# One hybrid mixer layer: order of the first loads, of the weight splits, and the way the modulation's row groups are summed

## The chip, the cores and the metric

One core of a Trainium2 chip. The metric is the device time of one execution in microseconds (us). It is given as the median of three runs, and a separate profiled execution gives the trace.

## What is computed

One layer in float32 with 1024 tokens of width 1024. From c comes a modulation, from x by RMS normalisation h; h is projected to all inputs of three mixers and to their gates:

```python
mod = jnp.einsum('bd,de->be', jax.nn.silu(c), w_ada) + b_ada
shift, scale, gate = jnp.split(mod[:, None, :], 3, axis=-1)
h = rms_norm(x, g_pre) * (1.0 + scale) + shift
proj = jnp.einsum('bsd,de->bse', h, w_in)
...
o_gla = rms_norm(o_gla, g_gla_norm.reshape(GLA_HEADS, GLA_VAL_DIM))
...
return x + gate * rms_norm(out, g_post)
```

The mixers are a forgetting attention (fox), a chunked gated linear attention (gla) and a causal pooling (pool). Each is gated, projected and merged, and one output projection follows.

## The kernel before

Every float32 matrix product is made of three matmuls (`mm3`, lines 143 to 145): operands are split in a high part rounded on ScalarE (line 109) and the rest, a subtraction on VectorE (line 111; both in `split`), and high by high, high by low and low by high are summed. A product of 128x512 in the text is one such matmul.

The kernel is written in a framework that orders the instructions of each engine itself by the program's order, its dependencies and priorities. So where lines are written is a wish; the order in which each engine gets its instructions is what the scheduler makes of it, and it may change far from the edited lines.

The start goes as follows. SyncE issues loads of 512 KB: `load_mod(0)`, the four tiles wa of the first modulation's weights (line 258), `load_x`, the eight tiles xn of x with 128 tokens each (line 274), and `start_w`, the weights wr_gq and wr_gk of the first two projections (line 278). `norm_x(g)` (lines 294 to 306) handles two tiles of x: sums of squares on ScalarE (line 301, Square) or VectorE (line 298), a root on ScalarE (line 303), a reciprocal and the scaling of xn on VectorE (lines 304, 306). `transpose_x` (lines 308 to 317) turns them on TensorE by 128x128 (line 313, into px) and copies to xT on ScalarE (line 315) or VectorE (line 317).

`gemv(j)` (lines 323 to 337) multiplies sc, the silu of c, by four tiles wa. It runs 32 matmuls of 256 columns (line 329) whose results stand in four groups of 32 equal rows of pr, one group for each of four parts of the sum. ScalarE copies pr to ar (line 332), and four matmuls with a column c32 of 1/32 (line 336) sum over all 128 rows, which adds the four groups, and turn the result into pt. `modulation(j)` adds biases and makes the shift and scale of two tiles of h, `gate(u)` those of the output's gate. `modulate(kt)` (lines 353 to 363) makes one tile of h for all tokens, hh (high) and hl (low), by a scale and shift on VectorE (line 361) and a split. `split_w` splits wr_gq and wr_gk into wh and wl; wnr is a third, narrow weight.

`first_products(kt)` (lines 412 to 419) multiplies tile kt of h with the three weights: 16 matmuls into ps_gq, ps_gk and ps_n. All eight tiles give 128. The next phase begins with ps_gv (lines 166 to 168), projections and then the gated linear attention in four units of `gla_unit`: matmuls psc (line 636) give scores, VectorE selects them into scs (lines 624, 628), and pso (line 658) multiplies them with the values. At a unit's end the sums of squares pm (line 694) go to VectorE (msq, line 696), and `rms_gla` (lines 700 to 713) takes a root on ScalarE, a reciprocal on VectorE (line 702) and splits the result rr into a high and a low part. The high part is multiplied by a selecting matrix into pb at line 710, the low part at line 711. Products of other projections (ps_zg, ps_fv, pp_zg) stand between them on TensorE wherever the scheduler put them.

Of the kernel before, what the change touches and what calls it, by code (L numbers as in the profile page):

```python
# [8 lines left out]
F32 = mybir.dt.float32  # L9
# [3 lines left out]
ALU = mybir.AluOpType  # L13
AX = mybir.AxisListType
PSUM = bass.MemoryType.PSUM

P = 128
# [12 lines left out]
def kernel(  # L30
# [22 lines left out]
    V, A, G, T = nc.vector, nc.scalar, nc.gpsimd, nc.tensor  # L53
# [9 lines left out]
    def open_pool(name, **kw):  # L63
        stack = ExitStack()
        return stack.enter_context(pool(name, **kw)), stack
# [7 lines left out]
    def halves():  # L73
        return ((0, slice(0, HALF)), (1, slice(HALF, S)))
# [7 lines left out]
    def bank(tag, name, shape=(P, HALF)):  # L82
        if tag == "acc":
            return ps_acc.tile(list(shape), F32, tag="acc", name=name, bufs=2)
        return ps_acc.tile(list(shape), F32, tag=tag, name=name, bufs=BANKS[tag])
# [18 lines left out]
    def const(shape, name, dt=F32):  # L104
        return cst.tile(shape, dt, tag=name, name=name)


    def split(raw, hi, lo, scale=1.0, E=None):
        i = A.activation(hi, raw, AF.Copy, scale=scale)  # L109
        if scale == 1.0:  # L110
            j = (E or V).tensor_tensor(out=lo, in0=raw, in1=hi.bitcast(F32), op=ALU.subtract)  # L111
        else:
            j = V.scalar_tensor_tensor(  # L113
                out=lo, in0=raw, scalar=scale, in1=hi.bitcast(F32), op0=ALU.mult, op1=ALU.subtract
            )
        return i, j
# [80 lines left out]
    ident = const([P, P], "ident")  # L197
    make_identity(nc, ident)
    c32 = const([P, 1], "c32")
# [8 lines left out]
    modc = const([P, 3, NK], "modc")  # L208
# [25 lines left out]
    st_pool, st_stack = open_pool("start", side="right")  # L234
# [16 lines left out]
    def load_wa(cols):  # L251

        parts = {}
        for z in range(2):
            for kh in range(2):
                t = sh((GT + ["t"] * 3 + XT[0:2])[ring[0] % 9], f"wa{len(wa)}{z}{kh}", (P, 4, 256))
                ring[0] += 1
                nc.sync.dma_start(t, w_ada[0, kh * 512 : (kh + 1) * 512, cols[z] : cols[z] + 256].rearrange(
                    "(k p) e -> p k e", p=P))
                parts[z, kh] = t  # L260
        wa.append(parts)

    def load_mod(j):

        load_wa((j * 256, D + j * 256))
# [6 lines left out]
    def load_x(a, b):  # L272
        for st in range(a, b):
            nc.sync.dma_start(xn[st], x[0, st * P : (st + 1) * P, :])

    def start_w(col, name, tags):
        raw = wtile(("wh", "wl")[name == "gk0"], f"wr_{name}", F32)
        nc.sync.dma_start(raw, w_in[0, :, col : col + P].rearrange("(k p) e -> p k e", p=P))
        hi = sh(tags[0], f"wh_{name}", (P, NK, P), F32R)
        lo = sh(tags[1], f"wl_{name}", (P, NK, P), F32R)  # L280
        return raw, hi, lo

    load_mod(0)
    load_x(0, 4)
    wq = start_w(C_GQ, "gq0", ("x3", "x4"))
    load_x(4, 8)
    wk = start_w(C_GK, "gk0", ("x5", "x2"))


# [3 lines left out]
    def norm_x(g):  # L293
        sl = slice(2 * g, 2 * g + 2)
        for st in (2 * g, 2 * g + 1):
            junk = hp.tile([P, D], F32, tag=f"hh{5 + st % 2}", name=f"junk{st}")
            if st in (3, 5, 7):
                V.tensor_tensor_reduce(out=junk, in0=xn[st], in1=xn[st], scale=1.0, scalar=0.0,
                                       op0=ALU.mult, op1=ALU.add, accum_out=ss[:, st : st + 1])
            else:  # L300
                A.activation(junk, xn[st], AF.Square, accum_out=ss[:, st : st + 1])
        V.tensor_scalar(out=ss[:, sl], in0=ss[:, sl], scalar1=1.0 / D, scalar2=EPS, op0=ALU.mult, op1=ALU.add)
        A.activation(ss[:, sl], ss[:, sl], AF.Sqrt)
        V.reciprocal(ss[:, sl], ss[:, sl])
        for st in (2 * g, 2 * g + 1):
            V.tensor_scalar(out=xn[st], in0=xn[st], scalar1=ss[:, st : st + 1], scalar2=None, op0=ALU.mult)

    def transpose_x(hf, k0, k1):
        hs = slice(hf * HALF, (hf + 1) * HALF)
        for kt in range(k0, k1):  # L310
            px = bank((("a", "a", "c", "c"), ("c", "c", "acc", "acc"))[hf][kt % 4], f"px{kt}{hf}")
            for j in range(4):
                T.transpose(px[:, j * P : (j + 1) * P], xn[4 * hf + j][:, kt * P : (kt + 1) * P], ident)
            if kt % 2 == 0:
                A.copy(xT[kt][:, hs], px)
            else:
                V.tensor_copy(xT[kt][:, hs], px)

    def split_w(w):
        raw, hi, lo = w  # L320
        split(raw, hi, lo)

    def gemv(j):

        pr = bank("b", f"pr{j}", (P, 2, 256))
        for z in range(2):
            for kh in range(2):
                for k in range(4):
                    T.matmul(pr[32 * k : 32 * k + 32, z, :], sc[:, 4 * kh + k : 4 * kh + k + 1].to_broadcast([P, 32]),  # L329
                             wa[j][z, kh][:, k, :], start=(kh == 0), stop=(kh == 1))  # L330
        ar = st_pool.tile([P, 4, P], F32, tag="ar", name=f"ar{j}", bufs=2)
        A.copy(ar, pr.rearrange("p z (c e) -> p (z c) e", e=P))

        pt = bank("d", f"pt{j}", (P, 4))
        for i in range(4):
            T.matmul(pt[:, i : i + 1], ar[:, i, :], c32, start=True, stop=True)
        return pt

    def modulation(j):
        pt = gemv(j)  # L340
        js = slice(2 * j, 2 * j + 2)
        mc = st_pool.tile([P, 2], F32, tag="mc", name=f"mc{j}", bufs=2)
        V.tensor_tensor(out=modc[:, 0, js], in0=pt[:, 0:2], in1=bsh[:, js], op=ALU.add)
        V.tensor_tensor(out=mc, in0=pt[:, 2:4], in1=bsc[:, js], op=ALU.add)
        V.tensor_tensor(out=modc[:, 1, js], in0=mc, in1=gpre[:, js], op=ALU.mult)

    def gate(u):
        pt = gemv(4 + u)
        us = slice(4 * u, 4 * u + 4)
        V.tensor_tensor(out=modc[:, 2, us], in0=pt, in1=bgt[:, us], op=ALU.add)  # L350
        V.tensor_tensor(out=modc[:, 2, us], in0=modc[:, 2, us], in1=gpost[:, us], op=ALU.mult)

    def modulate(kt):
        hh.append(hp.tile([P, S], F32R, tag=f"hh{kt}", name=f"hh{kt}"))
        hl.append(hp.tile([P, S], F32R, tag=f"hl{kt}", name=f"hl{kt}"))
        for hf, hs in halves():
            ht = xT[kt][:, hs]
            if kt == NK - 1:

                ht = st_pool.tile([P, HALF], F32, tag="ht", name=f"ht{hf}", bufs=2)  # L360
            V.tensor_scalar(out=ht, in0=xT[kt][:, hs], scalar1=modc[:, 1, kt : kt + 1],
                            scalar2=modc[:, 0, kt : kt + 1], op0=ALU.mult, op1=ALU.add)
            split(ht, hh[kt][:, hs], hl[kt][:, hs])
# [5 lines left out]
    cv, bsh, bsc, gpre = colv[:, 0:8], colv[:, 8:16], colv[:, 16:24], colv[:, 24:32]  # L369
# [2 lines left out]
    V.scalar_tensor_tensor(out=sc8, in0=th8, scalar=1.0, in1=cv, op0=ALU.add, op1=ALU.mult)  # L372
    V.tensor_scalar(out=sc, in0=sc8, scalar1=0.5, scalar2=None, op0=ALU.mult)
    V.tensor_scalar(out=bsc, in0=bsc, scalar1=1.0, scalar2=None, op0=ALU.add)
    modulation(0)
    for g in range(2):
        norm_x(g)
    transpose_x(0, 0, NK)
    for g in range(2, 4):
        norm_x(g)  # L380
    split_w(wq)
    transpose_x(1, 0, 2)
    modulate(0)
    split_w(wk)


# [34 lines left out]
    for kt in range(NK):  # L421
        if kt in (0, 2, 4):
            modulation(kt // 2 + 1)
        if kt == 0:
            load_mod(3)
        elif kt in (2, 4):
            load_gate(kt // 2 - 1)
        if kt in (5, 7):
            gate((kt - 5) // 2)
        if kt + 1 < NK:  # L430
            modulate(kt + 1)
        first_products(kt)
# [827 lines left out]
    for st in range(8):  # L1260
# [17 lines left out]
        r = yp.tile([P, 1], F32, tag="r", name=f"r{st}", bufs=2)  # L1278
# [44 lines left out]
```

## Time and profile before

| what | us |
|---|---|
| median of three runs (lowest, highest) | 1117.84 (1116.75, 1120.27) |
| profiled execution | 1116.32 |
| its span on the core | 1114.6 |
| TensorE busy in the span | 1067.6 |
| VectorE busy | 754.9 |
| ScalarE busy | 455.4 |
| GpSimd busy | 389.6 |

The mean granted clock of TensorE is 0.989 of full speed in the profiled execution. Times in a timeline are from the start of the span. The time of an execution is 1.7 us longer than its span. PE is TensorE, DVE VectorE, ACT ScalarE and POOL GpSimd; a row names output <- inputs, and a name's buffer numbers are left out.

### The profile page before, as it was taken

The numbers are of one execution on the slowest core, as the hardware profiler recorded it, in microseconds if no ns is written. First come the engines' busy times: TensorE is split into PE (matmuls) and PEld (weight loads), VectorE is DVE, ScalarE is ACT, GpSimd is POOL, SyncE is SP. The second block draws the span as 40 slices with busy tenths as digits, with TensorE's granted clock in tenths as the row PEclk, the third lists the DMA queues.
The fourth block names the chain that finished last, engine by engine and source line by source line (L and its number), as shares of the span: only waits on it lengthen the run. The fifth ranks groups of instructions, "written<-read, shape, count | busy, mean of one in ns | idle before, by whom it ended". The sixth has DMA issues, their size and how long they took to land.

```text
span 1114.6 us, 15450 instructions
## 1 busy us (share of the span) xinstructions
PE 1067.6 (96%) x5621; PEld 864.1 (78%) x5621; DVE 754.9 (68%) x1413; ACT 455.4 (41%) x859; POOL 389.6 (35%) x336
## 2 busy tenths in 40 slices
PE   4999999999999899899999999999999999999997
PEld 3679888988777788688888888887776776787886
DVE  5646979675698877987757566557675669487323
ACT  5335454443552433243434444435543337343111
POOL 1022326123075245445656454431210434343000
PEclk9999998999999999999999999999999899999999
DMA  9930110222142343146763334369969562464232
GB/s 316 306 106 6 54 39 22 67 66 74 49 130 72 137 169 113 38 162 238 255 214 113 114 118 129 113 156 346 262 201 279 208 174 86 162 216 141 77 113 76
DMA packets 97488, 159.26 MB, mean 143 GB/s; under 512 B 7978, under 2 KB 71036, under 8 KB 97412
## 3 DMA queue, kind: packets, MB, share of 16 engines
q1 hardware_dynamic: 97060, 157.47, 44.5%
q8 instruction: 44, 0.72, 0.3%
q10 hardware_dynamic: 352, 0.80, 0.2%
q14 instruction: 32, 0.26, 0.1%
HBM read 113.13 MB, written 45.13 MB: 142 GB/s over the span
## 4 chain that ended last, share of the span: by engine, by line
PE 71%; DVE 11%; DMA 10%; issue 2%; ACT 2%; POOL 2%; SPq 1%; DVEq 0%; ACTq 0%; POOLq 0%
PE pp_m L143 7%; PE pp_m L145 7%; PE pp_m L144 7%; PE pso L1275 3%; PE pso L1274 3%; PE po L1133 3%; PE pso L1273 3%; PE psy L143 2%; PE psy L145 2%; PE psy L144 2%; PE psc L636 2%; PE tp L1123 2%; PE ps_gv L168 1%; PE ps_gv L166 1%; PE ps_gv L167 1%
## 5 line engine op out<-in xcount | busy, mean ns | idle before, releaser
L143 PE MATMUL psy<-ogh,wh_y 128*128 128x512 f32 x192 | 76.2, 403 | 6.3 <-DMA ogh<-ogh_d 4.1
L145 PE MATMUL psy<-ogh,wl_y 128*128 128x512 f32 x192 | 74.5, 397 | 2.0 <-DVE wl_y L113 2.0
L144 PE MATMUL psy<-ogl,wh_y 128*128 128x512 f32 x192 | 76.0, 396 | 0.0
L143 PE MATMUL pp_m<-hh,w_m 128*128 128x512 f32 x192 | 74.7, 389 | 0.0
L144 PE MATMUL pp_m<-hl,w_m 128*128 128x512 f32 x192 | 74.7, 389 | 0.0
L145 PE MATMUL pp_m<-hh,w_m 128*128 128x512 f32 x192 | 74.7, 389 | 0.0
L111 DVE TENSOR_TENSOR w_m<-wr_m,w_m 128x512 fp32r<-128x512 f32 x36 | 42.8, 1193 | 41.6 <-ACT w_m L109 41.6
L1029 POOL TENSOR_SCALAR_AFFINE_SELECT Fd<-F 128x128 f32<-128x128 f32 x64 | 22.3, 353 | 128.1 <-DVE mx L1051 90.5
L1058 ACT ACTIVATE t<-t,ng 128x1024 f32<-128x1024 f32 (+3 forms) x64 | 49.6, 777 | 37.9 <-DVE ng L1056 35.1
L111 DVE TENSOR_TENSOR w_m<-S_m,w_m 128x512 fp32r<-128x512 f32 x48 | 57.2, 1221 | 3.3 <-ACT w_m L109 2.7
L770 POOL TENSOR_TENSOR sb<-hh,hl 128x512 f32<-128x512 f32 x16 | 23.5, 1493 | 100.6 <-PE pr L329 70.5
L1046 DVE CUSTOM_DVE_ANT_0 t<-psL,F 128x512 f32<-128x512 f32 (+2 forms) x80 | 41.2, 524 | 21.6 <-PE psL L1043 9.4
L547 POOL TENSOR_TENSOR e<-cum 128x256 f32<-128x256 f32 x24 | 19.4, 807 | 93.0 <-ACT ko L580 26.4
L1274 PE MATMUL pso<-wol,mh 128*128 128x512 f32 (+1 forms) x136 | 51.2, 377 | 0.0
L1273 PE MATMUL pso<-woh,mh 128*128 128x512 f32 (+1 forms) x136 | 51.2, 376 | 0.0
L1275 PE MATMUL pso<-woh,ml 128*128 128x512 f32 (+1 forms) x136 | 51.0, 376 | 0.0
L934 ACT ACTIVATE o_m<-o_m 128x512 f32<-128x512 f32 x48 | 29.0, 629 | 53.8 <-DVE o_m L835 31.5
L1277 DVE TENSOR_TENSOR yo<-pso,gb 128x512 f32<-128x512 f32 (+1 forms) x17 | 11.2, 661 | 55.6 <-ACT jk L1276 55.6
L143 PEld LDWEIGHTS psy<-ogh,wh_y 128*128 128x128 f32 x192 | 36.5, 191 | 15.0 <-DMA ogh<-ogh_d 4.4
L1125 ACT COPY PT<-tp 128x512 f32<-128x512 f32 (+1 forms) x64 | 31.6, 504 | 39.6 <-PE tp L1123 36.2
L1123 PE MATMUL tp<-ident,t 128*128 128x128 f32 x288 | 45.7, 280 | 1.9 <-ACT t L1058 1.1
L1133 PE MATMUL po<-PT,vf 128*64 128x256 f32 (+1 forms) x320 | 45.5, 366 | 0.0
(579 smaller groups left out, 3357.8 us busy)
## 6 DMA issues: line engine op xcount, KB each, us to landing
wa<-in_w_ada_dram SPq DMA_DIRECT2D x24, 512.0 KB, 7.2
wr_m<-in_w_in_dram SPq DMA_DIRECT2D x24, 512.0 KB, 3.7
m_d<-o_m SPq DMA_DIRECT2D x24, 512.0 KB, 8.2
m_in<-m_d SPq DMA_DIRECT2D x24, 512.0 KB, 5.4
xn<-in_x_dram SPq DMA_DIRECT2D x8, 512.0 KB, 8.4
kl<-fkl_d SPq DMA_DIRECT2D x16, 256.0 KB, 10.1
kk<-fkh_d SPq DMA_DIRECT2D x16, 256.0 KB, 5.8
F<-fc_d SPq DMA_DIRECT2D x8, 512.0 KB
```

What stands on the lines that cost most here:

```text
L111: j = (E or V).tensor_tensor(out=lo, in0=raw, in1=hi.bitcast(F32), op=ALU.subtract)
L143: T.matmul(ps, wh, rh, start=first, stop=False)
L144: T.matmul(ps, wh, rl, start=False, stop=False)
L145: T.matmul(ps, wl, rh, start=False, stop=last)
L1046: V.tensor_tensor_reduce(out=t[:, c0:e], in0=ps[:, : e - c0], in1=Fb[p, h][:, c0:e], scale=1.0, scalar=-3e38, op0=ALU.subtract, op1=ALU.ma ...
L1058: A.activation(t[:, :W], t[:, :W], AF.Exp, bias=ng[:, 0:1], accum_out=sm)
L1123: T.transpose(tp[:, j, :], t[:, kb * P : (kb + 1) * P], ident)
L1125: A.copy(pts[h, kg][:, 0:nb, qs], tp[:, 0:nb, :])
L1133: T.matmul(po[64 * h : 64 * h + 64, q0:256], vf[p // 2, kb // 4][:, kb % 4, col : col + 64], pts[h, kb // 4][:, kb % 4, q0:256], start=(kb ...
L1273: T.matmul(ps[:, :w], mh[k][:, sl], hi, start=(k == 0), stop=False)
L1274: T.matmul(ps[:, :w], mh[k][:, sl], lo, start=False, stop=False)
L1275: T.matmul(ps[:, :w], ml[k][:, sl], hi, start=False, stop=(k == NK - 1))
```

## The change

All eight tiles of x are loaded first, then the four wa, then wr_gq and wr_gk. In `gemv` four transposes take the place of the four matmuls with c32; the result, 128 columns for each of the four, is read by a reduction on VectorE that takes one column of every 32 and adds the four. In the program's order `transpose_x(1, 0, 2)`, `modulation(0)` and `modulate(0)` are written behind the normalisation of x, and both `split_w` behind `modulate(0)`.

```diff
--- before.py
+++ after.py
@@ -280,10 +280,9 @@
         lo = sh(tags[1], f"wl_{name}", (P, NK, P), F32R)
         return raw, hi, lo
 
+    load_x(0, 8)
     load_mod(0)
-    load_x(0, 4)
     wq = start_w(C_GQ, "gq0", ("x3", "x4"))
-    load_x(4, 8)
     wk = start_w(C_GK, "gk0", ("x5", "x2"))
 
 
@@ -331,18 +330,19 @@
         ar = st_pool.tile([P, 4, P], F32, tag="ar", name=f"ar{j}", bufs=2)
         A.copy(ar, pr.rearrange("p z (c e) -> p (z c) e", e=P))
 
-        pt = bank("d", f"pt{j}", (P, 4))
+        pt = bank("d", f"pt{j}", (P, 4, P))
         for i in range(4):
-            T.matmul(pt[:, i : i + 1], ar[:, i, :], c32, start=True, stop=True)
-        return pt
+            T.transpose(pt[:, i, :], ar[:, i, :], ident)
+        mc = st_pool.tile([P, 4], F32, tag="mc", name=f"mc{j}", bufs=2)
+        V.tensor_reduce(mc, pt.rearrange("p a (g r) -> p a g r", r=32)[:, :, :, 0], axis=AX.X, op=ALU.add)
+        return mc
 
     def modulation(j):
         pt = gemv(j)
         js = slice(2 * j, 2 * j + 2)
-        mc = st_pool.tile([P, 2], F32, tag="mc", name=f"mc{j}", bufs=2)
         V.tensor_tensor(out=modc[:, 0, js], in0=pt[:, 0:2], in1=bsh[:, js], op=ALU.add)
-        V.tensor_tensor(out=mc, in0=pt[:, 2:4], in1=bsc[:, js], op=ALU.add)
-        V.tensor_tensor(out=modc[:, 1, js], in0=mc, in1=gpre[:, js], op=ALU.mult)
+        V.tensor_tensor(out=pt[:, 2:4], in0=pt[:, 2:4], in1=bsc[:, js], op=ALU.add)
+        V.tensor_tensor(out=modc[:, 1, js], in0=pt[:, 2:4], in1=gpre[:, js], op=ALU.mult)
 
     def gate(u):
         pt = gemv(4 + u)
@@ -372,15 +372,15 @@
     V.scalar_tensor_tensor(out=sc8, in0=th8, scalar=1.0, in1=cv, op0=ALU.add, op1=ALU.mult)
     V.tensor_scalar(out=sc, in0=sc8, scalar1=0.5, scalar2=None, op0=ALU.mult)
     V.tensor_scalar(out=bsc, in0=bsc, scalar1=1.0, scalar2=None, op0=ALU.add)
-    modulation(0)
     for g in range(2):
         norm_x(g)
     transpose_x(0, 0, NK)
     for g in range(2, 4):
         norm_x(g)
+    transpose_x(1, 0, 2)
+    modulation(0)
+    modulate(0)
     split_w(wq)
-    transpose_x(1, 0, 2)
-    modulate(0)
     split_w(wk)
```

The first place is VectorE (DVE) around the weight splits and the first tiles of h. From line 283 on, lines of the changed kernel stand one higher or lower than before (L316 is L317 of before). Before (wl is the low part of a weight, xT the transposed x, hl the low part of h):

```order
L361 TENSOR_SCALAR xT_249<-xT_249,modc 128x512
L304 RECIPROCAL ss<-ss 128x2
L317 COPY xT_254<-px_342 128x512
L302 TENSOR_SCALAR ss<-ss 128x2
L306 TENSOR_SCALAR xn_221<-xn_221,ss 128x1024
L306 TENSOR_SCALAR xn_222<-xn_222,ss 128x1024
L111 TENSOR_TENSOR wl_gk_248<-wr_gk_245,wh_gk_247 128x1024
L317 COPY xT_256<-px_354 128x512
L111 TENSOR_TENSOR wnr<-wn,wnr 128x8x64
L111 TENSOR_TENSOR hl_393<-xT_249,hh_392 128x512
L304 RECIPROCAL ss<-ss 128x2
L306 TENSOR_SCALAR xn_223<-xn_223,ss 128x1024
```

After:

```order
L111 TENSOR_TENSOR wl_gq_244<-wr_gq_241,wh_gq_243 128x1024
L316 COPY xT_250<-px_356 128x512
L316 COPY xT_256<-px_463 128x512
L337 TENSOR_REDUCE mc_386<-pt_381 128x4
L111 TENSOR_TENSOR wl_gk_248<-wr_gk_245,wh_gk_247 128x1024
L316 COPY xT_254<-px_451 128x512
L343 TENSOR_TENSOR modc<-mc_386,colv 128x2
L344 TENSOR_TENSOR mc_386<-mc_386,colv 128x2
L111 TENSOR_TENSOR wnr<-wn,wnr 128x8x64
L345 TENSOR_TENSOR modc<-mc_386,colv 128x2
L361 TENSOR_SCALAR xT_249<-xT_249,modc 128x512 x2
L361 TENSOR_SCALAR xT_250<-xT_250,modc 128x512 x2
```

The scale and shift of the first tile of h (L361) stood among the scalings of x and ahead of wl_gk and wnr; now it stands behind wl_gq, wl_gk, wnr and the reduction L337, and nothing of x is left behind it.

The second place is ScalarE (ACT) at the start. Before:

```order
L247 ACT_TABLE_LOAD
L247 ACTIVATE th_215<-one_col 128x1
L370 ACTIVATE th_215<-colv 128x8
L301 ACTIVATE junk_294,ss<-xn_217 128x1024
L301 ACTIVATE junk_296,ss<-xn_218 128x1024
L332 COPY ar_283<-pr_266 128x512
L303 ACT_TABLE_LOAD
L303 ACTIVATE ss<-ss 128x2
L301 ACTIVATE junk_303,ss<-xn_219 128x1024
L109 ACTIVATE wh_gq_239<-wr_gq_237 128x1024
L303 ACTIVATE ss<-ss 128x2
L301 ACTIVATE junk_360,ss<-xn_221 128x1024
```

After:

```order
L247 ACT_TABLE_LOAD
L247 ACTIVATE th_215<-one_col 128x1
L300 ACTIVATE junk_266,ss<-xn_217 128x1024
L300 ACTIVATE junk_268,ss<-xn_218 128x1024
L302 ACT_TABLE_LOAD
L302 ACTIVATE ss<-ss 128x2
L300 ACTIVATE junk_275,ss<-xn_219 128x1024
L370 ACT_TABLE_LOAD
L370 ACTIVATE th_215<-colv 128x8
L300 ACTIVATE junk_332,ss<-xn_221 128x1024
L302 ACT_TABLE_LOAD
L302 ACTIVATE ss<-ss 128x2
```

Tanh of c (into th) stood ahead of the squares of x and shared the first table; now it stands between two roots (L302 after, L303 before), and two more table loads stand around it.

The third place is TensorE (PE) at the end of the gated linear attention, from the second of two matmuls pm to the first pb. Before, around pm:

```order
L143 MATMUL ps_zg001_2856<-hh6_731,wh_zg00_2823 128x512
L694 MATMUL pm11_2498<-o2111_2503,c32_181 32x512
L144 MATMUL ps_zg001_2856<-hl6_732,wh_zg00_2823 128x512
L145 MATMUL ps_zg001_2856<-hh6_731,wl_zg00_2824 128x512
L143 MATMUL ps_zg001_2856<-hh7_755,wh_zg00_2823 128x512
```

and around pb, 53 products behind that pm:

```order
L144 MATMUL ps_zg011_2922<-hl7_756,wh_zg01_2889 128x512
L145 MATMUL ps_zg011_2922<-hh7_755,wl_zg01_2890 128x512
L710 MATMUL pb20_2749<-rr1_2746,sel4_174 128x512
L710 MATMUL pb21_2753<-rr1_2746,sel4_174 128x512
L143 MATMUL pp1_zg1_3096<-hh4_621,w1_zg1_3061 128x512
L144 MATMUL pp1_zg1_3096<-hl4_622,w1_zg1_3061 128x512
L711 MATMUL pb20_2749<-rr1_2746,sel4_174 128x512
L711 MATMUL pb21_2753<-rr1_2746,sel4_174 128x512
```

After, around pm:

```order
L144 MATMUL ps_zg010_2901<-hl7_762,wh_zg01_2897 128x512
L694 MATMUL pm11_2506<-o2111_2511,c32_181 32x512
L145 MATMUL ps_zg010_2901<-hh7_761,wl_zg01_2898 128x512
L143 MATMUL ps_zg011_2930<-hh0_391,wh_zg01_2897 128x512
L144 MATMUL ps_zg011_2930<-hl0_392,wh_zg01_2897 128x512
```

and around pb:

```order
L144 MATMUL ps_zg011_2930<-hl7_762,wh_zg01_2897 128x512
L145 MATMUL ps_zg011_2930<-hh7_761,wl_zg01_2898 128x512
L710 MATMUL pb20_2757<-rr1_2754,sel4_174 128x512
L710 MATMUL pb21_2761<-rr1_2754,sel4_174 128x512
L143 MATMUL pp1_zg1_3104<-hh4_624,w1_zg1_3069 128x512
L144 MATMUL pp1_zg1_3104<-hl4_625,w1_zg1_3069 128x512
L143 MATMUL pp5_zg1_3171<-hh4_624,w5_zg1_3081 128x512
L144 MATMUL pp5_zg1_3171<-hl4_625,w5_zg1_3081 128x512
L711 MATMUL pb20_2757<-rr1_2754,sel4_174 128x512
L711 MATMUL pb21_2761<-rr1_2754,sel4_174 128x512
```

Between pm and pb there are 25 products now: the rest of ps_zg010 and all 24 of ps_zg011. The ps_zg001 products and most of ps_zg010 stand ahead of pm. Between pb's high part (L710) and its low part (L711) there are four products instead of two.

## Rows read from the trace of the kernel before

**Rows 1.** The page, part 4: the chain that ended last, by engine.

```profile
PE 71%; DVE 11%; DMA 10%; issue 2%; ACT 2%; POOL 2%; SPq 1%; DVEq 0%; ACTq 0%; POOLq 0%
```

**Rows 2.** PE's timeline, start us, length us, [idle before <-what ended it].

```profile
8.17 3.64 PE L329 MATMUL pr<-wa,sc 128*32 128x256 f32 x32 [1.00 <-DVE sc L373]
...
35.77 0.64 PE L329 MATMUL pr<-wa,sc 128*32 128x256 f32 x8 [0.95 <-DMA wa<-in_w_ada_dram]
36.34 1.97 PE L313 MATMUL px<-ident,xn 128*128 128x128 f32 x16
...
38.80 0.50 PE L418 MATMUL ps_n<-hh,wnr 128*128 128x512 f32 x1
...
56.10 1.93 PE L329 MATMUL pr<-wa,sc 128*32 128x256 f32 x32
```

**Rows 3.** Table of stretches: us, busy and (count) per engine, clock, DMA.

```profile
30.00:40.00 10.00, 8.31 (x73) 5.66 (x73) 7.07 (x17) 4.52 (x8) 0.00 (x0) 1.00 0.73 233
40.00:80.00 40.00, 40.00 (x264) 28.88 (x262) 18.29 (x37) 14.44 (x24) 4.55 (x4) 1.00 0.67 210
```

**Rows 4.** PE's timeline, later in the start.

```profile
50.58 0.95 PE L336 MATMUL pt<-c,ar 128*128 128x1 f32 x8
...
80.28 0.36 PE L166 MATMUL ps_gv<-wh_gv,hh 128*128 128x256 f32 x1
```

**Rows 5.** ACT's timeline, start.

```profile
13.68 1.28 ACT L303 ACT_TABLE_LOAD   x1
14.97 0.20 ACT L303 ACTIVATE ss<-ss 128x2 f32<-128x2 f32 x1
...
20.32 1.06 ACT L301 ACTIVATE junk<-xn 128x1024 f32<-128x1024 f32 x1 [0.66 <-DMA xn<-in_x_dram]
```

**Rows 6.** DVE's timeline, start.

```profile
15.21 0.17 DVE L304 RECIPROCAL ss<-ss 128x2 f32<-128x2 f32 x1 [1.82 <-ACT ss L303]
...
16.88 1.22 DVE L298 CUSTOM_DVE_ANT_0 junk<-xn 128x1024 f32<-128x1024 f32 x1
...
27.50 1.22 DVE L111 TENSOR_TENSOR wl_gk<-wr_gk,wh_gk 128x1024 fp32r<-128x1024 f32 x1
28.64 0.69 DVE L317 COPY xT<-px 128x512 f32<-128x512 f32 x1
...
30.64 1.42 DVE L306 TENSOR_SCALAR xn<-xn,ss 128x1024 f32<-128x1024 f32 x2
```

**Rows 7.** Table of stretches around four waits of PE, columns as in rows 3.

```profile
176.00:192.00 16.00, 13.93 (x77) 12.32 (x77) 15.77 (x21) 5.48 (x12) 10.36 (x8) 0.68 0.08 25
364.00:372.00 8.00, 6.37 (x21) 5.16 (x22) 6.65 (x10) 3.42 (x6) 1.76 (x2) 0.79 0.49 166
460.00:465.00 5.00, 2.84 (x13) 2.02 (x12) 5.00 (x8) 1.58 (x2) 2.75 (x2) 1.00 0.00 0
864.00:872.00 8.00, 6.64 (x19) 4.93 (x19) 2.32 (x10) 0.63 (x3) 0.68 (x1) 0.57 1.02 409
```

**Rows 8.** PE's timeline, four rows behind waits.

```profile
178.08 1.23 PE L658 MATMUL pso<-scs,vg 128*128 128x128 f32 x4 [2.07 <-DVE scs L628]
...
365.63 0.80 PE L143 MATMUL pp_zp<-T4h,w_zp 128*128 128x512 f32 x1 [3.88 <-DVE o_zp L967]
...
462.65 0.50 PE L143 MATMUL pspl<-dh,wph 128*128 128x512 f32 x1 [2.16 <-ACT dh L109]
...
865.36 0.79 PE L143 MATMUL psy<-ogh,wh_y 128*128 128x512 f32 x1 [4.06 <-DMA ogh<-ogh_d]
```

**Rows 9.** DVE's timeline, end of the gated linear attention.

```profile
281.28 0.69 DVE L696 TENSOR_SCALAR msq<-pm 64x512 f32<-64x512 f32 x1 [7.96 <-PE pm L694]
...
286.83 3.35 DVE L702 RECIPROCAL msq<-msq 128x512 f32<-128x512 f32 x1
```

**Rows 10.** PE's timeline, the same place.

```profile
280.20 1.04 PE L694 MATMUL pm<-o,c 128*32 128x512 f32 x2
...
293.31 0.62 PE L710 MATMUL pb<-rr,sel 128*128 128x512 f32 x2
```

## The prediction

> **What bounds the kernel now.** I read the chain of waits first: TensorE (PE) is 71% of it, VectorE (DVE) 11%, DMA 10% [rows 1]. So only two kinds of place matter: the start, before PE has a dense stream, and the few places where PE stands and waits. Then I read PE's timeline from 0 to 81 us. The reader is to see single groups with gaps up to the row that starts at 38.80, and after it 512-column products one after the other [rows 2]. By the table of stretches PE is busy 8.31 of 10 us from 30 to 40, and 40.00 of 40 from 40 to 80 [rows 3]. The first product of the next phase (ps_gv) starts at 80.28 [rows 4]. So what the start is worth is when that dense stream begins, and how long it then is.
>
> **The change part by part.**
>
> *Loads.* SyncE issued four wa, four x, one w, four x, one w, 512 KB each; now eight x, four wa, two w. Nothing is added, from the 14th issue on the queue is as before. The twelfth transfer of before is the seventh x tile, on which ScalarE (ACT) waited until 20.32 [rows 5]. Now the twelfth is the last wa, so the first modulation can be summed at about 20.4 instead of 12, while x is complete at about 14 instead of 21 or 22. Modulation was not what was late before; the second half of x was: its last scaling ran on DVE at 30.64 for 1.42 (two tiles), behind wl_gk at 27.50 [rows 6], and PE's transposes of it and then the products followed.
>
> *What bounds the first product now.* The order on DVE (shown ahead) has, between its first scaling of x and the first tile of h: eight scalings at 0.71 (5.7 us), three row sums at 1.22 and their reads (3.9), eight copies of transposes at 0.65 (5.2), wl_gq and wl_gk at 1.22 each, wnr at half of that (0.6), and some fifteen small ones at 0.15 or so (2.2) [rows 6]: 20 us. So on DVE the splits stand ahead of the first tile, though the code writes them behind it. DVE can begin when the first two x tiles have landed (at about 8.0 and not much later, since PE ran on wa, then the first in the queue, from 8.17 [rows 2]) and ACT has squared them, loaded its table and taken the root: 2 x 1.06 + 1.28 + 0.2 [rows 5] and two small steps, so about 12.3. 12.3 + 20 = 32.3, then one modulation step and its split on ACT, by half of wl_gk 0.6 each, the first of them counted with the small ones: first product at about 33, where the dense stream of before began at 38.8. Bounds: 31 (if none of the small ones costs anything) and 36 (if DVE waits in between; before has one wait of 1.82 at the first reciprocal [rows 6]).
>
> *What is in the dense stream.* Before: 80.28 - 38.80 = 41.5. Now added: the three products that stood earlier (0.7) and three quarters of a gemv more (112 of its matmuls stood in the stream, now 136; 32 take 1.93 [rows 2], so 1.4). Taken away: a pt was eight passes of one column, 0.95 us [rows 4]; now it is four transposes, by those of x (16 in 1.97 us [rows 2]) 0.48. Four stood in the stream, five do now: 3.6 - 2.4 = 1.2 less. The new sum on DVE over 128x4 is one small step, 0.17 by its neighbours; it is beside PE, and what it delays is the second pair of h tiles, ahead of which 34 products (7.7 us) now stand. Sum: 41.5 + 0.7 + 1.4 - 1.2 = 42.4, and 33 + 42.4 = 75.4, so **-4.9** at ps_gv. Bounds: -0.9 (a start at 36, and 1 us more for a late wa piece, of which before has a wait of 0.95 at 35.77 [rows 2]) and -6.9 (a start at 31).
>
> *ACT's tables.* Tanh of c is now taken between two roots, so ACT loads a table twice more: 1.28 each [rows 5], so 2.6 us. ACT waited for x in these microseconds anyway (0.66 us at the row of 20.32), and DVE's 20 us begin before either of them. I cost them at nothing, since DVE has its own work queued meanwhile; uncovered they cost 2.6. The Trainium skill (ScalarE: Activation LUTs, Table sets) has a rule against just this, to batch activations by table set, and prices a switch at 2.66 us with a drain (What ACT_TABLE_LOAD costs); by it the two would be 5.3 us on ACT. The trace shows the 1.28 with the root at its end (13.68 and 14.97), and no drain, so the row is taken.
>
> *The middle of the gated linear attention, 160 to 200 us.* Here DVE is the late one: busy 15.77 of 16 us over 176 to 192 [rows 7]. PE waits 2.07 us for the selected scores up to 178.08 [rows 8], and the granted clock is 0.68 in the mean over these 16 us, between its levels of 2.4 and 1.2 GHz: 16 x 0.32 = 5.1 lost, or some 10 us at half rate. PE arriving 5 us earlier finds DVE advanced too, but DVE has no spare time, and the order moves ten to twenty filler products ahead of the scores. The price lies between -5.1 (no drop of the clock) and +4 (all the gain waits again). I take **+1.2**: a wait or two of 1 us more, at nearly the same drop.
>
> *The tail of that phase, where I see a new wait.* From the second pm (280.20) DVE runs a chain: mean square 281.28, eight splits T2l and T3l of 0.6, reciprocal 286.83 for 3.35 [rows 9]; ACT's rr, which the first pb needs, follows the reciprocal. In before the pb came at 293.31 with no gap, because the pm (1.0) and 53 products lay between: (293.31 - 280.20 - 1.0) / 53 = 0.228 each [rows 10]. The order of after has **25** products there. 1.0 + 25 x 0.228 = 6.7, but rr's high part is ready only with the reciprocal's end (290.18) and a split of 0.6 on ACT: 10.6 after the pm. PE waits 10.6 - 6.7 = **+3.9**. Behind it, two pb and four products (1.4 us) lead to L711, which needs rr's low part; on DVE four hl splits (before: three) stand ahead of that: 290.1 + 4 x 0.6 + 0.69 = 293.2, 13.0 after the pm, while PE comes at 12.0: **+1.0**. DVE and ACT in this chain are in the same order otherwise. Bounds: 0 (if PE is held up earlier, so that the chain starts earlier against it) and +6.
>
> *The clock after that wait.* PE idled 3.88 us up to 365.63 [rows 8]; the stretch 364 to 372 has a granted clock of 0.79 [rows 7]: 8 x 0.21 = 1.7 lost. After 2.16 us up to 462.65 the clock stays at 1.00 [rows 7, 8]. A wait of 3.9 is nearest to the first: **+1.7**; bounds 0 and 5.1 (as at 178). The Trainium skill says that waits of PE in the middle of a kernel bring the half rate back (TensorE: Matmul & The Clock Gate, HAM oscillation); the rows agree for the waits at 178 and 365, and not for the one at 462.
>
> From about 310 us on, the order of PE is the same in both, so what stands there is carried to the end. **Sum: -4.9 + 1.2 + 3.9 + 1.0 + 1.7 = +2.9** on the profiled execution's 1116.3: 1119.2. That execution stands 1.5 below the runs' median of 1117.84; on the median it would be 1120.7. I give 1119.2, since the profiled one is what was summed.
>
> **The rivals.** 0.3% (3.35 us) is about what a measurement of this kernel can tell from no change: faster is under 1114.5, slower over 1121.2.
>
> A. *The start's gain is kept.* PE is held at the scores by DVE a little longer, and the chain to rr then starts earlier against PE's 25 products, or the clock doesn't fall at 178, which is worth 5.1. For it: PE is the chain's 71%, and a wait in the middle takes away the later one. Against it: the chain from pm to rr is local, and does not depend on what was before the pm. -4.9 + 1.2 + 1.0 = -2.7 with the pb wait hidden, -4.9 - 5.1 + 6.6 = -3.4 with no drop at 178; with both -4.9 - 5.1 + 1.0 = -9.0. So 1107 to 1113.6, its nearer end the likelier.
>
> B. *Slower: both waits drop the clock for long.* The mechanism is the wait at the first pb, if it draws the price of the gap of 4.06 us that ends at 865.36 [rows 8]: 864 to 872 has 0.57 [rows 7], 8 x 0.43 = 3.4 lost. It decides from a start of the products at 33.5 or later, or from a middle of +2. Then -4.9 + 2 + 3.9 + 1.0 + 3.4 = +5.4: 1121.7, with the start's own bound up to 1123.
>
> C. *The start does not gain.* The table loads and the late modulation (20.4 us) push h back: first product at 36, 36 + 42.4 - 80.3 = -1.9, with the tail's waits as they are: -1.9 + 1.2 + 6.6 = +5.9, 1122.2. It is also the case in which the splits' move does the opposite of what is written, since the order has wl_gk ahead of the first tile's modulation now, and had it behind. By the Trainium skill's 5.3 us (ScalarE: Activation LUTs, What ACT_TABLE_LOAD costs) in full the first product would come at about 38, and the sum at +8. Against it: DVE, not ACT, has the 20 us.
>
> **How the numbers follow.** My forecast (the start's gain eaten by the tail, -2 to +4.9 on the profiled time, 1114.3 to 1121.2) 0.48; A 0.22; B 0.18; C 0.12. Range 1112.0 to 1122.8: it leaves out the far end of A, and of B and C what is above their sums. Chances: faster is nearly all of A, 0.22; slower is most of B and C and a little of the forecast's upper end, 0.30; same 0.48.
>
> **What would show it.** Right: first ps_gv at 74 to 77 us; two more ACT_TABLE_LOAD before 25 us; a PE gap of 3 to 5 us in front of pb L710 near 290 us, ended by ACT's rr, and granted clock 0.5 to 0.8 in the next 4 us; a PE wait on scs of 1 to 3 us between 170 and 185. Wrong: ps_gv at 78 or later (C); no gap at L710 (A); a clock of 1.00 over 176 to 190 (A).

## The result, and the profile after

The changed kernel takes 1127.21 us in the median of nine runs (1123.22 to 1133.83). The kernel before takes 1118.92 in nine runs of the same comparison. The ratio is 1.008, with a 95% interval of 1.0062 to 1.0098: slower, by 8.3 us in the medians, where +2.9 was forecast with 1122.8 as the upper end. The profiled execution of the changed kernel is 1127.21 long, its span 1125.5.

The page of the changed kernel, the rows of PE and of the chain that ended last (part 1, part 4):

```profile
PE 1067.0 (95%) x5597; PEld 861.2 (77%) x5597; DVE 758.4 (67%) x1419; ACT 457.9 (41%) x861; POOL 390.4 (35%) x336
...
PE 65%; DVE 15%; DMA 11%; issue 3%; POOL 3%; ACT 3%; SPq 0%; DVEq 0%; ACTq 0%; POOLq 0%
```

PE is as busy as before (1067.6 then) in a span that is 10.9 longer. So nothing was added to PE's work: it waits more. PE's share of the chain falls from 71% [rows 1] to 65%, and DVE's rises from 11% to 15%.

PE's timeline of the changed kernel at the places of the prediction (start us, length us, engine, line, and in brackets the idle time before the row and what ended it):

```profile
31.86 0.80 PE L143 MATMUL ps_gq<-hh,wh_gq 128*128 128x512 f32 x1 [1.60 <-ACT hh L109]
...
75.37 0.36 PE L166 MATMUL ps_gv<-wh_gv,hh 128*128 128x256 f32 x1
...
171.78 0.68 PE L636 MATMUL psc<-qbd,ko 128*128 128x128 f32 x4 [1.72 <-DVE scs L624]
...
174.43 0.71 PE L658 MATMUL pso<-scs,vg 128*128 128x128 f32 x4 [1.04 <-DVE scs L628]
...
184.37 0.71 PE L658 MATMUL pso<-scs,vg 128*128 128x128 f32 x4 [4.21 <-DVE scs L628]
...
297.64 1.07 PE L710 MATMUL pb<-rr,sel 128*128 128x512 f32 x2 [3.76 <-ACT rr L109]
...
319.22 0.50 PE L145 MATMUL pp_zg<-T3h,w_zg 128*128 128x512 f32 x1 [0.42 <-DVE w_zg L111]
```

The start came as forecast: the first product at 31.86 (forecast 33), and ps_gv at 75.37 where 80.28 was [rows 4] and 75.4 was forecast. The gap ahead of pb is there too, 3.76 us (forecast 3.9). What was not forecast in its size are the three waits for DVE's selected scores, 1.72, 1.04 and 4.21 us, where before has the single 2.07 [rows 8]. The last row is a product whose wait (0.4 us) and place are the same in all kernels of this study; now it starts at 319.22, and in the kernel before at 312.93:

```profile
312.93 0.50 PE L145 MATMUL pp_zg<-T3h,w_zg 128*128 128x512 f32 x1 [0.41 <-DVE w_zg L111]
```

The stretches behind the two long waits, and the start of the dense stream (us, busy and count of each engine, clock, DMA):

```profile
31.00:36.00 5.00, 4.14 (x17) 2.56 (x18) 4.20 (x9) 2.19 (x4) 0.00 (x0) 0.66 0.61 198
184.00:192.00 8.00, 7.63 (x37) 6.84 (x38) 7.91 (x14) 3.29 (x7) 2.12 (x2) 0.57 0.26 72
298.00:302.00 4.00, 3.92 (x11) 2.56 (x10) 4.00 (x8) 1.81 (x4) 0.00 (x0) 0.59 0.03 8
```

After the wait of 4.21 the granted clock is 0.57 over 8 us, so 3.4 us are lost, where before lost 5.1 over 176 to 192 [rows 7]. After the wait at pb it is 0.59 over 4 us: 1.6 lost, forecast 1.7.

DVE's timeline says why the scores came late. In the changed kernel, between the two pairs of last selections (L628) of the second gated-linear-attention unit:

```profile
173.07 1.30 DVE L628 COPY_PREDICATED scs<-gmask,psc 128x256 f32<-128x256 uint32 x2
174.40 1.52 DVE L475 TENSOR_TENSOR lfl<-lfl,lfa 8x1024 f32<-8x1024 f32 x1
175.96 1.01 DVE L551 TENSOR_TENSOR kt<-gk,e 128x512 f32<-128x512 f32 x1
176.89 2.96 DVE L562 TENSOR_TENSOR qbd<-gq,e 64x256 f32<-64x256 f32 x2
179.87 2.28 DVE L491 TENSOR_TENSOR_SCAN fcum<-one_col,lfl 8x1024 f32<-8x1024 f32 x1
182.19 0.93 DVE L773 TENSOR_TENSOR sb<-sb 128x512 f32<-128x512 f32 x1
183.04 1.28 DVE L628 COPY_PREDICATED scs<-gmask,psc 128x256 f32<-128x256 uint32 x2
```

and the same pairs in the kernel before:

```profile
176.75 1.28 DVE L628 COPY_PREDICATED scs<-gmask,psc 128x256 f32<-128x256 uint32 x2
178.06 1.22 DVE L474 SCALAR_TENSOR_TENSOR lfl<-lrf,lfl 8x1024 f32<-8x1024 f32 x1
179.30 1.31 DVE L628 COPY_PREDICATED scs<-gmask,psc 128x256 f32<-128x256 uint32 x2
```

Before, one instruction stands between the pairs. Now there are six (five rows, one of them of two): a step of the forget logs and the scan fcum (L475, L491), kt and qbd of the next unit (L551, L562), a sum of h's halves (L773). They fill 8.7 us; 2.1 of these are the two qbd, which take 2.96 here and take 0.84 in the kernel before, at 185.36 there. PE's queue has pso with the second pair ahead of other products, so it stands still until 184.37.

The chain to rr, on DVE of the changed kernel, answers to [rows 9]:

```profile
288.03 0.69 DVE L696 TENSOR_SCALAR msq<-pm 64x512 f32<-64x512 f32 x1 [11.78 <-PE pm L694]
...
293.58 3.35 DVE L702 RECIPROCAL msq<-msq 128x512 f32<-128x512 f32 x1
296.84 2.43 DVE L111 TENSOR_TENSOR hl<-sb,hh 128x512 fp32r<-128x512 f32 x4
```

From msq to the reciprocal's start it is 5.55 us, as before (286.83 - 281.28), and four hl splits now stand ahead of rr, as the order had shown.

### The profile page after: what moved, and what is told of

It reads as the page before. It is cut to its first block, busy times and chain, and to the rows that moved or that the text cites. A ratio compares the mean times of both kernels' runs of the same rounds, so it can differ in the third digit from the quotient of the medians.

```text
span 1125.5 us, 15408 instructions
## 1 busy us (share of the span) xinstructions
PE 1067.0 (95%) x5597; PEld 861.2 (77%) x5597; DVE 758.4 (67%) x1419; ACT 457.9 (41%) x861; POOL 390.4 (35%) x336
## 4 chain that ended last, share of the span: by engine, by line
PE 65%; DVE 15%; DMA 11%; issue 3%; POOL 3%; ACT 3%; SPq 0%; DVEq 0%; ACTq 0%; POOLq 0%
PE pp_m L145 6%; PE pp_m L143 6%; PE pp_m L144 6%; PE pso L1275 3%; PE po L1133 3%; PE pso L1274 3%; PE pso L1273 3%; PE psy L143 2%; PE psy L145 2%; PE psy L144 2%; PE psc L636 2%; PE tp L1123 2%; PE ps_gv L167 1%; PE ps_gv L168 1%; PE ps_gv L166 1%
```

## The experiments

All were timed against the kernel before, in comparisons of their own (its median there: 1118.92 for the changed kernel, 1119.41 for the first four experiments, 1118.38 for the last three). "Row T3h" is the product that starts at 312.93 before and at 319.22 in the changed kernel. The change of its start is the sum of three: the change of ps_gv's start (80.28 before), of the stretch from there to PE's arrival at pb, without a gap ahead of pb (213.0 before), and of the stretch from that arrival to row T3h (19.6 before). These columns come from one profiled execution of each kernel.

| kernel | first ps_gv | ps_gv to pb, to before | pb to row T3h, to before | row T3h, to before | median | ratio (95%) |
|---|---|---|---|---|---|---|
| changed kernel | 75.37 | +5.5 | +5.7 | +6.3 | 1127.21 | 1.008 (1.0062 to 1.0098) |
| loads alone | 76.09 | -1.2 | 0.0 | -5.4 | 1115.04 | 0.9961 (0.9941 to 0.998) |
| transposes alone | 77.95 | +6.2 | +5.5 | +9.4 | 1129.39 | 1.0101 (1.0076 to 1.0127) |
| changed, tail pinned | 76.66 | +4.7 | 0.0 | +1.1 | 1120.34 | 1.0011 (0.9988 to 1.0034) |
| changed, middle pinned | 75.87 | +0.4 | 0.0 | -4.0 | 1116.22 | 0.9984 (0.9967 to 1.0002) |
| loads, Tanh early | 76.26 | -1.2 | 0.0 | -5.2 | 1113.6 | 0.9961 (0.9943 to 0.998) |
| loads, splits behind | 76.29 | -1.3 | 0.0 | -5.3 | 1113.85 | 0.996 (0.9942 to 0.9979) |
| loads, both | 75.64 | -1.3 | 0.0 | -5.9 | 1113.57 | 0.996 (0.9938 to 0.9982) |

The change of the median follows row T3h within 2 us in every row of the table. So nearly all of the time is won and lost ahead of 320 us. Behind it the profiled executions take 801.7 (before) to 809.9 us (middle pinned), the changed kernel 806.3 and the loads alone 806.7. So the changed kernel's longer rest there is no loss of its own. The runs of one kernel differ as much: before alone goes from 1112.5 to 1122.63.

The third part of the change needs no run. Without it (loads and transposes alone) PE, DVE and ACT get the same instructions in the same order as in the changed kernel; only the numbers in tile names differ. Written order is a wish here, and this one changed nothing.

**Loads alone.** The kernel before with this edit:

```diff
-    load_mod(0)
-    load_x(0, 4)
+    load_x(0, 8)
+    load_mod(0)
     wq = start_w(C_GQ, "gq0", ("x3", "x4"))
-    load_x(4, 8)
```

> The kernel before with the new load order alone (eight x, four wa, two w); row sums by c32 and the splits' place as before. Theory (the transposes set off the reshuffle of the later order; the loads bring the gain): first ps_gv at 76 to 78 us, a little behind the changed kernel's 75.37 since five pt cost 0.95 each, no PE gap ahead of pb L710, a wait on scs near 2 us as before, 3 to 5 us faster than before. Rival (the loads do the harm, by two more table loads and a late modulation, and by what they shift later): as slow as the changed kernel, about 1127, with its 4.2 us wait on scs and its 3.8 us gap ahead of pb.

Measured: 0.9961, 4.4 us faster. PE's timeline:

```profile
76.09 0.36 PE L166 MATMUL ps_gv<-wh_gv,hh 128*128 128x256 f32 x1
...
173.88 0.71 PE L657 MATMUL pso<-scs,vg 128*128 128x128 f32 x4 [2.06 <-DVE scs L627]
...
287.89 0.62 PE L709 MATMUL pb<-rr,sel 128*128 128x512 f32 x2
```

The wait on scs is 2.06, as before, and no gap stands ahead of pb; its order has 53 products between pm and pb, as before. The loads bring 4.2 of the changed kernel's 4.9 us at ps_gv, the two extra table loads included, and none of the harm.

**Transposes alone.** The edit of `gemv` and `modulation` as in the change, on the kernel before.

> The kernel before with the row sums by transposes and the reduction alone; loads and splits as before. Theory: first ps_gv within 2 us of 80.3, but the waits of the changed kernel: 3 to 5 us on scs and 3 to 4 us ahead of pb L710; 6 to 12 us slower than before, so about as slow as the changed kernel or slower. Rival (the loads do the harm): within 2 us of before, no gap ahead of pb.

Measured: 1.0101, 10 us slower, though ps_gv comes 2.3 us earlier. PE's timeline:

```profile
186.97 1.22 PE L659 MATMUL pso<-scs,vg 128*128 128x128 f32 x4 [4.22 <-DVE scs L629]
...
300.90 1.22 PE L711 MATMUL pb<-rr,sel 128*128 128x512 f32 x2 [3.76 <-ACT rr L109]
```

Both are the waits of the changed kernel to 0.01 us (L711 here is L710 there). So the part of the change that looks smallest, four transposes and a reduction for four one-column products, carries all the harm (this run does not split the transposes from the reduction), and it does so 100 us and more behind its last place (ahead of ps_gv): with it the scheduler puts the later instructions in another order. Its order has 25 products between pm and pb, with the loads or without.

**Tail pinned.** The changed kernel with one ordering edge (`after` sets an order for the scheduler and no wait; pms holds the last pm of each unit):

```diff
-                mm3(ps, wh[:, k, :], wl[:, k, :], hh[k][:, hs], hl[k][:, hs], k == 0, k == NK - 1)
+                m = mm3(ps, wh[:, k, :], wl[:, k, :], hh[k][:, hs], hl[k][:, hs], k == 0, k == NK - 1)
+                if name == "zg01" and i == 0 and k == 0:
+                    after(m, pms[3])
```

> The changed kernel with one ordering edge without a wait: the first product of ps_zg010 stays behind the last pm L694, so 48 products instead of 25 stand between pm and pb L710. Theory: the gap ahead of pb goes (below 0.5 us), and with it the half clock behind it; 4 to 6 us faster than the changed kernel if nothing else waits before pm in its place. Rival (the gap only moves, since the products that filled the time ahead of pm are now missing there): a new PE wait of 2 to 5 us ahead of pm, and a time within 2 us of the changed kernel's.

Measured: 1120.34, 6.9 us faster than the changed kernel in the medians, and 5.2 us by row T3h. No gap stands ahead of pb any more, and none took its place ahead of pm. The wait in the middle is untouched:

```profile
185.70 1.22 PE L662 MATMUL pso<-scs,vg 128*128 128x128 f32 x4 [4.22 <-DVE scs L632]
...
294.41 0.61 PE L715 MATMUL pb<-rr,sel 128*128 128x512 f32 x2
```

So the tail's order costs 5 to 7 us (5.7 by the stretch from pb to row T3h), and with it alone repaired the kernel is about where before was: the start's gain (-3.6 here) and the middle's loss (+4.7) nearly cancel.

**Middle pinned.** The changed kernel with ordering edges on DVE behind the last selection of unit 01 (last_sel):

```diff
-        V.tensor_tensor_scan(out=fcum[r8, :], data0=one_col[r8, :].to_broadcast([8, S]), data1=lf, initial=0.0,
+        i = V.tensor_tensor_scan(out=fcum[r8, :], data0=one_col[r8, :].to_broadcast([8, S]), data1=lf, initial=0.0,
                              op0=ALU.mult, op1=ALU.add)
+        after(i, last_sel["01"])
...
+        if uid == "10_64":
+            after(i, last_sel["01"])
...
-    forget_logs()
     gla_unit(0, 1)
+    forget_logs()
...
-            after(i, mark[0])
+            after(i, last_sel["01"])
```

The second piece stands behind kt and behind each qbd of unit 10, the last behind the first of the sums sb.

> The changed kernel with ordering edges on DVE: the last selection of scores of unit 01 comes ahead of the scan fcum, of the first kt and qbd of unit 10 and of the sums sb, as it does in the kernel before; the order on PE then has 53 products between pm and pb again. Theory: wait on scs back to about 2 us or less, no gap ahead of pb, first ps_gv at 75.4 as in the changed kernel: 3 to 6 us faster than before. Rival (the loss comes from elsewhere, such as the waits behind 372 us, which are 4.8 us longer in the changed kernel's profile than in the profile before): still 3 us or more slower than before.

Measured: 1116.22, 0.9984 (0.9967 to 1.0002): 3.2 us below before in the median, with an interval that just touches no change. PE's and DVE's timelines:

```profile
171.58 0.68 PE L643 MATMUL psc<-qbd,ko 128*128 128x128 f32 x4 [1.50 <-DVE scs L631]
...
176.82 0.71 PE L666 MATMUL pso<-scs,vg 128*128 128x128 f32 x4 [0.34 <-DVE scs L635]
...
184.32 0.49 PE L671 MATMUL pso<-qe,S 64*128 64x128 f32 x4 [2.98 <-DVE S L685]
...
289.31 0.62 PE L718 MATMUL pb<-rr,sel 128*128 128x512 f32 x2
```

```profile
171.23 1.36 DVE L635 COPY_PREDICATED scs<-gmask,psc 128x256 f32<-128x256 uint32 x2
...
175.45 1.31 DVE L635 COPY_PREDICATED scs<-gmask,psc 128x256 f32<-128x256 uint32 x2
```

The selections are now 4.2 us apart (it was 10), the wait on them is 0.34, but 1.50 us at psc stay, and a new wait of 2.98 on the state S (L685), which the pinned instructions now delay. The order behind changed too: 53 products stand between pm and pb again, and no gap there. So this run repairs both places, and its median can't say what the middle is worth alone; against the run with the tail pinned it is 4.1 us. The trace splits it: from ps_gv to pb it takes 213.4 us, where the changed kernel takes 218.5, so 5.1 of the middle's 5.5 are gone, new waits included.

**Tanh early.** The loads alone, and Tanh ahead of the first root on ACT:

```diff
-    A.activation(th8, cv, AF.Tanh, scale=0.5)
+    th_i = A.activation(th8, cv, AF.Tanh, scale=0.5)
...
-        A.activation(ss[:, sl], ss[:, sl], AF.Sqrt)
+        i = A.activation(ss[:, sl], ss[:, sl], AF.Sqrt)
+        if g == 0:
+            after(i, th_i)
```

> The load order alone (first experiment) with one more ordering edge: Tanh of c comes ahead of the first root on ACT, so the two extra table loads go. Theory (the two loads of 1.28 us stand in the chain ACT root, DVE reciprocal and scaling, so they cost part of the start): first ps_gv 0.5 to 2 us ahead of the first experiment's 76.09, and 0 to 2 us faster than its 1115. Rival (they are hidden beside DVE's own work, as the prediction had it): first ps_gv within 0.3 us of 76.1.

Measured: ps_gv at 76.26, so the rival's number holds, but not its reason. The two loads are gone and the first product comes at 31.10, 0.5 earlier, but PE then waits for the second modulation's weights:

```profile
27.92 0.64 PE L330 MATMUL pr<-wa,sc 128*32 128x256 f32 x8 [0.46 <-DMA wa<-in_w_ada_dram]
30.53 0.64 PE L330 MATMUL pr<-wa,sc 128*32 128x256 f32 x8 [1.97 <-DMA wa<-in_w_ada_dram]
```

Behind these waits the granted clock is 0.57 over 32 to 36 us, 1.7 us lost, where it is 1.00 with the loads alone. So this run shows that taking the table loads away gains nothing here; what they would cost without these two losses is not shown.

**Splits behind.** The loads alone, and wl_gk and wnr on DVE really behind the first tile of h (firsts holds the instructions of scale and shift, in order):

```diff
-    split_w(wk)
+    after(split_w(wk)[1], firsts[1])
...
-    split(wn, wnr[:, :, 0:64], wnr[:, :, 64:128])
+    after(split(wn, wnr[:, :, 0:64], wnr[:, :, 64:128])[1], firsts[1])
```

> The load order alone with two ordering edges on DVE: the low parts wl_gk and wnr come behind the scale and shift of the first tile of h, as the change's text has it and its instruction order has not. Theory (DVE's list ahead of the first tile sets the first product): first product 1 to 2 us ahead of the 31.61 of the first experiment, first ps_gv 0.5 to 2 us ahead of 76.09. Rival (what PE or ACT does then is late instead, or the narrow weight's products wait for wnr): first ps_gv within 0.3 us of 76.1.

Measured: the first product comes at 30.18, 1.4 earlier as expected, and ps_gv at 76.29 all the same: PE waits later in the stream.

```profile
30.18 0.50 PE L143 MATMUL ps_gq<-hh,wh_gq 128*128 128x512 f32 x1 [0.90 <-ACT hh L109]
...
54.18 0.50 PE L143 MATMUL ps_gq<-hh,wh_gq 128*128 128x512 f32 x1 [1.28 <-ACT hh L109]
```

That wait is for ACT by name, and for a transfer behind it. On ACT the four hh stand behind wh_gv, whose raw weights arrive only at 52.55; DVE's input to the hh (xT, line 362) came from 49.83 on:

```profile
52.55 1.06 ACT L109 ACTIVATE wh_gv<-wr_gv 128x1024 fp32r<-128x1024 f32 x1 [8.50 <-DMA wr_gv<-in_w_in_dram]
53.52 2.18 ACT L109 ACTIVATE hh<-xT 128x512 fp32r<-128x512 f32 x4
```

**Both.**

> Both edges together on the load order alone. Theory: the two gains add, first ps_gv 1 to 4 us ahead of 76.09 and 1112 to 1115 us in all. Rival: the second is hidden once the first is made, or a DMA (the second modulation's weights) ends the wait of PE instead: no more than the better of the two alone.

Measured: ps_gv at 75.64, 0.45 ahead of the loads alone, and the same ratio, 0.996. The first product is at 29.12, 2.5 earlier, and DMA waits of 0.72 and 0.79 us follow behind it. In these three runs a transfer takes over as soon as the start gets shorter elsewhere: the second modulation's weights with Tanh early, wr_gv with the splits behind. The loads alone, and each of these three, are 4.4 to 4.8 us faster than the kernel before and 12 or more faster than the changed one; they can't be told from each other, so the single edit is the one to keep.

## Why the prediction was wrong

- **Start, -4.9.** The number is right, 75.37 - 80.28 = -4.9, in part by luck: its inner account was off, with errors that cancel. The first x tile was there by 4.42, since ACT squared it then, and not at about 8; DVE began to scale at 8.67 and not at 12.3. But DVE also waited 3.8 us in between, 0.86 for th and 1.04 for a root, both behind the extra table loads, and 1.89 for PE:

```profile
9.49 1.28 ACT L370 ACT_TABLE_LOAD   x1
...
12.05 1.28 ACT L302 ACT_TABLE_LOAD   x1
13.35 0.20 ACT L302 ACTIVATE ss<-ss 128x2 f32<-128x2 f32 x1
```

  The first product came at 31.86 and not at 33, and the stream from it to ps_gv took 43.5 us and not 42.4, with 1.7 us lost to a granted clock of 0.66 over 31 to 36, for which the sum had no term. So the table loads did stand in the chain, as rival C had it, and DVE's own work did not hide them, though the prediction took it to. In the run with Tanh early, where ps_gv comes no sooner without them (76.26 against 76.09), the waits for weights and the lower clock took their place. The Trainium skill's drain behind a load (ScalarE: Activation LUTs, What ACT_TABLE_LOAD costs) is not in these rows either: the load at 12.05 takes 1.28, and the root starts at 13.35.
- **Middle, +1.2.** This is the step that failed. From ps_gv to PE's arrival at pb it took 213.0 us before (80.28 to 293.31), with no gap at its end, and 218.5 now (75.37 to 297.64 - 3.76), for the same work: +5.5. Of this 4.9 are waits (1.72 + 1.04 + 4.21 against 2.07) and 0.6 is PE's busy time. The prediction said that PE would arrive earlier at a DVE without spare time, and bounded the loss by the gain of the start. It read the new order on PE there, and DVE's only at the start and in the tail. But DVE's order had moved in the middle too, with 8.7 us of work for later steps between the two pairs of selections, so the bound of +4 did not hold. With the old order of the selections (middle pinned) the stretch takes 213.4.
- **Tail, +3.9 and +1.0.** The mechanism was right: 3.76 us, from 25 counted products, ended by rr on ACT. The further 1.0 at L711 did not come, since PE ran the four products ahead of it at half clock.
- **Clock behind it, +1.7.** 1.6 by the table of stretches. From PE's arrival at pb to row T3h the two last terms together are 6.29 - 0.57 - 3.76 = +2.0, forecast 2.7.
- **The base.** The sum was made on a profiled execution of 1116.3, and the forecast was put there. The median of before is 1118.9 in nine runs, 2.6 above it, and all of that went into the miss. Set on the median, +2.9 would have given 1121.8.

Of the 8.0 us between 1119.2 and 1127.2, 4.3 are the middle and 2.6 the base; -0.9 is the tail with its clock. The remaining 2.0 lies behind 320 us, where the order is the same and executions differ by more than that; no run here splits it.

Rival A (no gap at pb) and rival C (ps_gv late) are out by the rows above. Rival B named the right side, with the wait at pb at a longer loss of clock; the loss was the short one, and the middle brought what B lacked.

What is shown: the loads bring most of the gain, the edit of the transposes brings the loss, and two places of the order carry it, since pinning them takes it away. Left open: why the scheduler's order turns on that edit, and on which piece of it, the transposes or the reduction; no run varied what it weighs.

## What to carry to other kernels

Where a scheduler orders the engines, price an edit in its whole order, not at its place: here a small edit ahead of 80 us cost 10 us at 180 and 290. Compare the order of every engine at each place where PE waits for another, count the work that stands between a producer's instructions and the filler that covers each chain, and pin those places with ordering edges before judging the edit itself. Put a forecast on the median of the runs; the profiled execution is one draw.

## What was not expected of the hardware

- DVE instructions of one form took very different times. The two qbd at 176.89 took 2.96 together while POOL was busy 3.57 of 4 us from 176 to 180, and the same form took 0.85 for two at 184.95. In the kernel before, ek took 1.67 at 174.48, and 0.68 in the changed kernel at 168.65. How busy POOL is does not tell slow from fast, since POOL is busy 1.83 of 2 us from 168 to 170 too, beside the fast ek. What differs is which engine began first. Ahead of the slow ek POOL's sb had begun (171.96 for 3.64), and ahead of the slow qbd too; beside the fast ek POOL's e began 0.23 later. And el, 0.16 at 176.67 before, took 1.26 in the changed kernel and ended with POOL's sb:

```profile
165.72 2.99 POOL L770 TENSOR_TENSOR sb<-hh,hl 128x512 f32<-128x512 f32 x2 [6.68 <-DVE qbd L586]
...
176.38 3.18 POOL L770 TENSOR_TENSOR sb<-hh,hl 128x512 f32<-128x512 f32 x2
```

```profile
167.48 1.26 DVE L602 COPY el<-ec 128x4 f32<-128x4 f32 x1
168.65 0.68 DVE L604 TENSOR_TENSOR ek<-cum 128x512 f32<-128x512 f32 x1
```

  That a POOL instruction under way holds these DVE instructions up fits the rows and was not tested.
- The clock's fall did not follow from the wait alone. Behind a wait of 1.60 us at 31.86 the changed kernel's granted clock is 0.66 over 31 to 36 (the table above); with the loads alone the same wait is 1.59, the clock is 1.00 over 31 to 36, and the second product lasts 0.40 where that of the changed kernel at 32.45 lasts 0.63 (rows below). The changed kernel's PE had waited 0.55 more at 29.63, which the loads alone have not. But with the tail pinned PE waits 1.54 up to 30.75 and 0.52 up to 31.91, and the clock is 1.00 over 31 to 36 as well. So no rule for the fall comes out of these rows:

```profile
31.61 0.50 PE L143 MATMUL ps_gq<-hh,wh_gq 128*128 128x512 f32 x1 [1.59 <-ACT hh L109]
31.94 0.40 PE L143 MATMUL ps_gk<-hh,wh_gk 128*128 128x512 f32 x1
```
